# Expert stage: every low part on VectorE, a 16-bit one-hot, and gate and up weights loaded as pairs of rows

## The chip, the cores and the metric

One core of one Trainium2 chip runs the whole program in one launch. The metric is the device time of an execution in microseconds, as the median of the runs shown. TensorE multiplies, VectorE and ScalarE work on tiles in SBUF and PSUM, GpSimd works on tiles in SBUF and issues the indirect DMAs, SyncE issues the plain loads and stores. In the profile they are PE (with PEld for its weight loads), DVE, ACT, POOL and SP.

## The reference

Two encoder layers (`DEPTH = 2`) on 1024 tokens of 1024 features, all float32. Each layer has three sub-layers, each added to its scaled input and normalised: a parallel token mixer (grouped-query attention, a gated long convolution, latent attention), a cross-attention into 256 memory tokens, and the mixture of experts that this document is about:

```python
def expert_choice_moe(x, w_router, w_gate, w_up, w_down):
    cap = EC_FACTOR * n_tok // N_EXPERTS                        # 2 * 1024 // 16 = 128
    aff = jax.nn.softmax((x @ w_router).astype(jnp.float32), axis=-1)
    gates, idx = lax.top_k(aff.transpose(0, 2, 1), cap)         # each expert chooses 128 tokens
    xe = jax.vmap(lambda xb, ib: xb[ib])(x, idx)
    hid = jax.nn.silu(einsum(xe, w_gate)) * einsum(xe, w_up)    # [128, 1024] @ [1024, 512], twice
    ye = einsum(hid, w_down) * gates[..., None]                 # [128, 512] @ [512, 1024]
    return zeros.at[idx].add(ye)
```

Sixteen experts per layer; their weights (gate, up and down, 6 MB per expert) are each read once.

## The kernel before

Each float32 product is made of three passes over operands that are split exactly in two parts of 12 bits (`mm3`, L186): high x high, high x low, low x high. A `Weight` (L122) is a block of 512 KB: it is loaded by SyncE when it is made, and when first asked for (`get`) it is split: ScalarE copies it into the high part, and VectorE or GpSimd subtracts that from the raw block, which gives the low part (`split`, L174 to L177). The argument `le` says which of the two makes the low part.

An expert has eight blocks of gate and up (four units `u`, with `i` = 0 for gate and 1 for up, each 256 of the 1024 rows; two blocks of 128 rows lie side by side in a partition, `k` = 2) and four of down (two units of two blocks of 128 rows). `GP` and `DP` (L51, L52) give one of the eight and one of the four to GpSimd. `expert_units` (L1527) is the order of the blocks: gate and up 0, gate and up 1, down 0 of the expert before, gate and up 2, down 1 of the expert before, gate and up 3. The order of the instructions on TensorE, VectorE and ScalarE is the order in which the program writes them. `take` (L1575) hands out the next block; each call also splits the block that lies three (`SPLIT`, four from expert 8 on) ahead, and makes new blocks, that is, issues their loads, as long as the raw and split ones count less than 37 (`DEEP`). All these tiles share one pool of 41 buffers of 4 KB per partition (`NA`, `big`).

The tokens of an expert: `route` (L1457) leaves for every token and expert the slot 1 to 128, or 0 (`pos`). `chosen` (L1504) makes the one-hot [token, tile, slot] of an expert by comparing a row of slot numbers with `pos`. `pick` (L1512) multiplies it, as the stationary operand, by a payload of five columns (token tile, token, three parts of the affinity), and so finds the 128 token numbers (`ix`) and gates (`gt`). `gather` (L1555) then has GpSimd fetch the 128 rows by an indirect DMA. `turn` (L1570) transposes them in eight steps of TensorE (`turn_tile`, L1363) and splits them (`xt`). `gu` (L1585) multiplies, and makes the hidden values after unit 3; `hidden` (L1600) transposes and splits those (`ht`), one unit later; `down` (L1608) multiplies by down, scales by the gate and has GpSimd add the rows into DRAM by an indirect DMA.

In the loop over units, `chosen` for the expert after next comes first in unit 0, ahead of that unit's products and of `hidden`; `gather` for it comes behind unit 1, `turn` for the next expert behind unit 2 (L1644 to L1661).

`places` (L1561) uses the last expert's one-hot once more, at the end of the last layer.

Of the kernel before, what the change touches and what calls it, by code (L numbers as in the profile page):

```python
# [50 lines left out]
GP = lambda u, i: "p" if i and u == 1 else "v"  # L51
DP = lambda u, i: "p" if i and u else "v"  # L52
CHP = 0
TP = 0
# [18 lines left out]
# ---------------------------------------------------------------- constants of the shapes  # L73
# [47 lines left out]
# ---------------------------------------------------------------- the kernel  # L121
class Weight:  # L122
    """A block of weights: loaded when made, split in two parts when first asked for."""
# [15 lines left out]
class Net:  # L139
# [10 lines left out]
    # ---- tiles  # L150
# [22 lines left out]
    # ---- common steps  # L173
    def split(self, h, l, src, le="v"):  # L174
        """src = h + l exactly, each part of 12 bits."""
        self.nc.scalar.activation(h, src, AF.Copy)  # L176
        (self.nc.vector if le == "v" else self.nc.gpsimd).tensor_sub(l, src, h.bitcast(F32))  # L177
# [14 lines left out]
    def bcast(self, row, n, name):  # L192
        """A row of DRAM on every partition."""
        t = self.big((128, n), name=name) if n > 512 else self.cp.tile([128, n], F32, name=name, tag=name)
        self.nc.sync.dma_start(t, bass.AP(tensor=row.tensor, offset=row.offset, ap=[[0, 128], [1, n]]))
        return t
# [18 lines left out]
    def tables(self):  # L215
# [7 lines left out]
        self.iota = cp.tile([128, CAP], F32, name="iota")  # L223
        nc.sync.dma_start(self.iota, bass.AP(tensor=A["k_iota"].tensor, offset=A["k_iota"].offset, ap=[[0, 128], [1, CAP]]))
# [7 lines left out]
    # ---- activations to [feature, token], split  # L232
# [3 lines left out]
    def to_T(self, T, pair, xs):  # L236
        """Two token tiles into the split, transposed activations."""
# [23 lines left out]
    # ---- input projection  # L261
    def rms_rope(self, P, nt, nh, cs, up="p"):
        """P [128 tok, nt, nh * 64] in PSUM, nt * nh = 8 -> normed and rotated in SBUF; cs [128, nt, 2, 64] has the
        gain in."""
# [29 lines left out]
    def rope_gain(self, l):  # L294
        """Rotary tables with the norm's gain (and, for q, the score's scale) in."""
# [22 lines left out]
    def in_proj(self, l, T, fill=iter(())):  # L318
# [16 lines left out]
        # latents  # L335
# [42 lines left out]
        # gated convolution's branches, [channel, token]  # L378
# [45 lines left out]
        # keys and values, then queries  # L424
# [71 lines left out]
    def rope_small(self, dst, src, nh, t, eng=None):  # L496
        """Rotary of 32 features: dst, src [128, nh, 32]."""
# [13 lines left out]
    # ---- attention over the tokens  # L511
    def mix_dst(self, f, *halves):
        """The place of feature f in the mixed features: (partition, block of 128)."""
# [6 lines left out]
    def scores(self, passes):  # L520
        """One query tile's scores [query, key]."""
# [9 lines left out]
    def exps(self, S, nm, den):  # L531
        """exp(score - max) in SBUF, and its sums."""
# [13 lines left out]
    def values(self, O, PH, PL, rd, V, half):  # L546
        """[value features: (high | low), 256 queries | 1 / sums] in PSUM, in two steps."""
# [22 lines left out]
    def attention(self, n_pairs, pair, side, lead=3):  # L570
        """pair(n): (token pair, passes(t), V(kt), feature); scores run ahead of the products with the
        values; side(n) emits other work between."""
# [55 lines left out]
    def latents(self, l):  # L628
        """The latent heads' queries, keys and values, split, to DRAM."""
# [69 lines left out]
    def mla(self, l):  # L699
        """The latent heads' pairs, and the steps that bring their keys, values and queries back."""  # L700
# [36 lines left out]
    # ---- long convolution  # L737
    def sin_reduced(self, dst, P, freq, fb):
        """dst = sin(freq * (P + b)), the argument brought into [-pi, pi]; in steps."""
# [20 lines left out]
    def filter_mlp(self):  # L760
        """Both layers' filter networks: layer l on the partitions [64 l, 64 l + 64)."""
# [22 lines left out]
        # the last hidden values' two parts, one layer's on all the partitions: (high, low), (low, high)  # L784
# [22 lines left out]
    def dft_step(self, r, tabs, cH, cL, sH, sL, free=False):  # L807
        """[128 k, (cos | sin), k tile, 256]: cosine sums of one input, sine sums of the other."""
# [19 lines left out]
    def filter_spectra(self):  # L828
        """Both layers' filters by their networks' last hidden values, transformed, to DRAM."""
# [207 lines left out]
    # ---- projection, residual, layer norm  # L1037
    def stats(self, r, st, i):
        """The statistics of half a tile."""
# [22 lines left out]
    def out_weights(self, W, ks):  # L1062
        """Rows of an output projection, by blocks of 128."""
        return [Weight(self, W[k * 128:(k + 1) * 128, :], (128, 1024), "wo", "p" if k % 2 else "v") for k in ks]

    def split_pair(self, raw, p):
        """Two token tiles of the mixed features in two parts."""
# [8 lines left out]
    def proj_ln(self, raw, ws, res, g, b, emit, turned, per=2, bg=iter(())):  # L1076
        """emit(t, tile) for LayerNorm(alpha * res + raw^T @ W); turned(i) later, for the
        transposes of every per tiles."""
# [68 lines left out]
    # ---- cross attention  # L1147
# [7 lines left out]
    def mem_turned(self, ms):  # L1155
        """The memory, transposed and split."""
# [14 lines left out]
    def mem_k(self, l):  # L1171
        """The memory's keys [feature, memory], split, to DRAM."""
# [29 lines left out]
    def mem_v(self, l):  # L1202
        """The memory's values [memory, feature], split, to DRAM."""
# [158 lines left out]
    # ---- expert choice  # L1362
    def turn_tile(self, x, H, L, le="v"):  # L1363
        """A token tile, transposed and split, in two steps."""
        for g in range(2):
            pt = self.psT((128, 4, 128))
            for k in range(4):
                j = g * 4 + k
                self.nc.tensor.transpose(pt[:, k, :], x[:, j * 128:(j + 1) * 128], self.ident)  # L1369
# [12 lines left out]
    def router(self, w, X, t):  # L1382
        """Affinities [token, expert] of a token tile."""
# [21 lines left out]
    def combine(self, x, z, Y, X, rows, n, m):  # L1405
        """n pairs of runs of m in order, x's and z's, into runs of 2 * m, or of the largest CAP: in Y or X, the one
        that holds them first. X may be x."""
# [15 lines left out]
    def rank(self, t0, n, top=None):  # L1423
        """The largest CAP, in order, of n token tiles' affinities and of top: [expert, CAP]. Each quarter of the
        tokens is put in order on its own partitions."""
# [31 lines left out]
    def route(self, bg):  # L1457
        """From the affinities [token, tile, expert] each expert's CAP tokens: their slots (from 1) by token,
        0 for those not chosen, and the payload that finds token and gate."""
        nc, cp = self.nc, self.cp  # L1460
        aff = self.aff[:, :, 0:16]
        # payload: token tile, token, and the affinity in three exact parts
# [8 lines left out]
        # the smallest of the largest CAP  # L1471
# [11 lines left out]
        # those above it, and those at it, with their ranks by token: all of those above come first  # L1483
# [16 lines left out]
        self.pos = cp.tile([128, 8, 16], F32, name="pos", tag="pos")  # L1500
        nc.vector.tensor_tensor(self.pos, w[:, 0], w[:, 1], OP.add)
        yield

    def chosen(self, e):  # L1504
        """An expert's tokens, one-hot: [token, tile, slot]."""
        nc = self.nc
        oh = self.tp.tile([128, 8, CAP], BF16, tag="m", name="oh", bufs=3)
        (nc.gpsimd if CHP and e > 1 else nc.vector).tensor_tensor(oh, self.iota.unsqueeze(1).to_broadcast([128, 8, CAP]),
                                self.pos[:, :, e:e + 1].to_broadcast([128, 8, CAP]), OP.is_equal)
        return oh  # L1510

    def pick(self, e, oh):  # L1512
        """An expert's tokens and gates, [slot, 1]."""
        nc = self.nc
        P = self.psT((128, 8))
        for t in range(NT):
            nc.tensor.matmul(P[:, 0:5], oh[:, t, :], self.payload[:, t, e, :], start=t == 0, stop=t == NT - 1)
        v = self.sml(8, "pv")
        nc.scalar.activation(v[:, 0:5], P[:, 0:5], AF.Copy)
        ix = self.sp.tile([128, 1], U32, tag="ix", name="ix", bufs=6)  # L1520
        nc.vector.scalar_tensor_tensor(ix, v[:, 0:1], 128.0, v[:, 1:2], op0=OP.mult, op1=OP.add)
        gt = self.sp.tile([128, 1], F32, tag="gt", name="gt", bufs=6)
        nc.vector.tensor_tensor(gt, v[:, 2:3], v[:, 3:4], OP.add)
        nc.vector.tensor_tensor(gt, gt, v[:, 4:5], OP.add)  # L1524
# [414 lines left out]
```

## Time and profile before

| | us |
|---|---|
| median of three runs | 2776.77 |
| lowest, highest | 2771.78, 2776.84 |
| profiled execution, first to last instruction (its own time) | 2770.1 |
| TensorE busy, VectorE busy in it | 2576.6, 2006.3 |
| ScalarE busy, GpSimd busy | 1575.2, 989.5 |
| layer 1's expert stage, from expert 0's hidden transposes to expert 15's | 295.2 |
| layer 2's | 295.0 |

The profile records no separate device time for the profiled execution beside its span. The span lies 1.7 us below the lowest of the three runs and 6.7 below the median. Engine times are sums over the whole span. A row of the timeline is an instruction, or several alike that follow each other (xN): its start from the beginning of the span, its duration, the engine, the line, the operation, and out<-in by the program's names. Successive instructions of one engine overlap a little, so that what an instruction costs its engine is the distance from start to start. L176 and L177 are the helper `split`: its instructions are told apart by the tiles (`egh`, `egl` high and low part of a gate or up block, `edh`, `edl` of a down block, `xt` of the tokens, `ht` of the hidden values). TensorE's matmuls are pipelined and overlap by nearly half of what the profile shows as their duration.

### The profile page before, as it was taken

The page shows a single profiled execution, that of the slowest core. Times are in us where ns is not written, and L with a number is a line of the kernel's source. Part 1 is how long each engine was busy: PE and PEld are TensorE (multiplying, and loading weights), DVE is VectorE, ACT ScalarE, POOL GpSimd, SP SyncE. Part 2 cuts the span into 40 slices and gives each one's busy share as a digit, 9 for nine tenths or more (in the row PEclk, how much of TensorE's full clock was granted, in tenths as well). Part 3 has the DMA queues.
Part 4 walks back from the last instruction along what each step waited for, and adds up shares of the span by engine and source line. Part 5 has one row for each costly group of instructions (what it writes and reads, how often), then busy time and mean ns, then how long its engine had stood idle before and what let it go on. Part 6 is the DMA issues. An engine that isn't in the chain of part 4 may idle for free. (4 is left out here: it accounts for less than half of the span.)

```text
span 2770.1 us, 39879 instructions
## 1 busy us (share of the span) xinstructions
PE 2576.6 (93%) x14484; PEld 2153.2 (78%) x14484; DVE 2006.3 (72%) x3040; ACT 1575.2 (57%) x2740; POOL 989.5 (36%) x831
## 2 busy tenths in 40 slices
PE   7999989999999995999989998999989999599998
PEld 5788879888778884777779887988977888477775
DVE  6665568877643578999976556887765357899997
ACT  4533359878223444787754425887831344377775
POOL 2443428742201201444451333774230130144444
PEclk9999999999999997999999999999999999799999
DMA  7546110233223357999885611024322235799994
GB/s 200 176 162 205 39 46 31 92 99 115 83 78 101 99 199 264 347 376 358 298 255 165 220 47 46 30 94 99 84 84 99 85 98 183 253 348 369 363 315 152
DMA packets 224566, 468.05 MB, mean 169 GB/s; under 512 B 27001, under 2 KB 83919, under 8 KB 224368
## 3 DMA queue, kind: packets, MB, share of 16 engines
q1 hardware_dynamic: 197504, 369.32, 38.5%
q0 software_dynamic: 22256, 79.40, 10.4%
q10 hardware_dynamic: 4608, 16.78, 1.5%
q8 instruction: 114, 1.87, 0.3%
q14 instruction: 84, 0.69, 0.1%
HBM read 378.66 MB, written 86.77 MB: 168 GB/s over the span
## 5 line engine op out<-in xcount | busy, mean ns | idle before, releaser
L177 DVE TENSOR_TENSOR egl<-eg,egh 128x1024 fp32r<-128x1024 f32 x224 | 315.4, 1436 | 32.7 <-ACT egh L176 27.2
L176 ACT ACTIVATE egh<-eg 128x1024 fp32r<-128x1024 f32 x256 | 267.8, 1058 | 82.4 <-DVE edl L177 40.9
L528 DVE TENSOR_REDUCE nm<-S 128x1 f32<-128x1024 f32 x192 | 234.1, 1221 | 96.6 <-PE S L525 95.6
L177 DVE TENSOR_TENSOR PL<-T,PH 128x512 fp32r<-128x512 f32 x384 | 246.0, 682 | 17.5 <-ACT PH L176 15.4
L176 ACT ACTIVATE PH<-T 128x512 fp32r<-128x512 f32 x384 | 209.8, 595 | 80.4 <-PE T L542 79.3
L534 ACT ACTIVATE E<-S,nm 128x1024 f32<-128x1024 f32 x192 | 214.5, 1117 | 11.5 <-DVE nm L528 9.6
L189 PE MATMUL S<-egl,xt 128*128 128x512 f32 x512 | 206.9, 404 | 8.6 <-DVE egl L177 6.3
L188 PE MATMUL S<-woh,mh 128*128 128x512 f32 x512 | 207.7, 406 | 6.3 <-DVE r L1107 6.3
L542 PE MATMUL T<-ident,E 128*128 128x128 f32 x1536 | 204.5, 274 | 5.7 <-DVE PL L177 4.8
L542 PEld LDWEIGHTS T<-ident,E 128*128 128x128 f32 x1536 | 178.2, 141 | 40.1 <-DVE PL L177 14.9
L189 PE MATMUL S<-wol,mh 128*128 128x512 f32 x512 | 202.2, 395 | 3.7 <-POOL wol L177 2.5
L188 PE MATMUL S<-egh,xt 128*128 128x512 f32 x512 | 204.9, 400 | 0.0
L190 PE MATMUL S<-egh,xt 128*128 128x512 f32 x512 | 201.5, 394 | 0.0
L190 PE MATMUL S<-woh,ml 128*128 128x512 f32 x512 | 201.3, 393 | 0.0
L567 POOL TENSOR_TENSOR olo<-olo 64x256 f32<-64x256 f32 x96 | 70.2, 731 | 290.5 <-ACT olo L565 286.6
L1616 PE MATMUL O<-edh,ht 128*128 128x512 f32 x512 | 156.9, 409 | 13.4 <-DVE ht L177 12.0
L525 PE MATMUL S<-KS,QS 128*128 128x512 f32 x512 | 147.1, 411 | 0.7 <-ACT E L534 0.7
L176 ACT ACTIVATE edh<-ed 128x1024 fp32r<-128x1024 f32 x128 | 133.6, 1055 | 23.1 <-PE O L1616 16.6
L552 PE MATMUL O<-PH,VS 128*128 128x256 f32 x512 | 137.9, 302 | 0.0
L189 PEld LDWEIGHTS S<-egl,xt 128*128 128x128 f32 x512 | 97.0, 189 | 47.3 <-DVE egl L177 21.5
L177 DVE TENSOR_TENSOR edl<-ed,edh 128x1024 fp32r<-128x1024 f32 x96 | 129.1, 1359 | 1.2 <-ACT edh L176 1.0
L1558 POOL DMA_INDIRECT xg<-x2d,ix x32 | 54.6, 1705 | 208.0 <-DVE gt L1524 121.4
(410 smaller groups left out, 7371.6 us busy)
## 6 DMA issues: line engine op xcount, KB each, us to landing
eg<-moe_w_gate SPq DMA_DIRECT2D x128, 512.0 KB, 8.1
eg<-moe_w_up SPq DMA_DIRECT2D x128, 512.0 KB, 8.8
ed<-moe_w_down SPq DMA_DIRECT2D x128, 512.0 KB, 5.6
tab<-k_dft POOLq DMA_DIRECT2D x24, 512.0 KB, 4.6
wv<-xa_wkv SPq DMA_DIRECT2D x16, 512.0 KB
wk<-xa_wkv SPq DMA_DIRECT2D x16, 512.0 KB, 6.6
tab<-k_idft POOLq DMA_DIRECT2D x16, 512.0 KB, 4.7
wo<-w_o SPq DMA_DIRECT2D x16, 512.0 KB, 3.6
```

The source lines that it names most:

```text
L176: self.nc.scalar.activation(h, src, AF.Copy)
L177: (self.nc.vector if le == "v" else self.nc.gpsimd).tensor_sub(l, src, h.bitcast(F32))
L188: mm(out, ah, bh, start=start, stop=False)
L189: mm(out, ah, bl, start=False, stop=False)
L190: mm(out, al, bh, start=False, stop=stop)
L525: self.nc.tensor.matmul(S[:, hf * 512:hf * 512 + 512], a, b[hf], start=n == 0, stop=n == len(passes) - 1)
L528: self.nc.vector.tensor_reduce(nm, S, axis=AX.X, op=OP.max, negate=True)
L534: self.nc.scalar.activation(E, S, AF.Exp, bias=nm, scale=1.0, accum_out=den)
L542: self.nc.tensor.transpose(pt[:, k, :], P[:, kt * 128:(kt + 1) * 128], self.ident)
L552: nc.tensor.matmul(O[:, :256], v, PH[half][:, k, :], start=kt == 0, stop=False)
L567: nc.gpsimd.tensor_tensor(lo[s, 0], lo[s, 0], lo[s, 1], OP.add)
L1616: nc.tensor.matmul(O[e][n], a[:, 2 * u + f, :], w[:, n * 512:n * 512 + 512], start=s, stop=z)
```

## The change

Four things change, all in the expert stage:

- `GP` and `DP` go; the low part of every block of expert weights is made by VectorE.
- The slot numbers (`iota`, each written twice side by side) and `pos` become bfloat16 tiles, laid out so that the one-hot is [token, slot, tile] with pairs of tiles as the innermost dimension of all three operands. The picks (and `places`) take their stationary operand from it with a step of eight elements. The gate is summed by ScalarE (`accum_out`) and no longer by two additions on VectorE. `chosen` moves behind `hidden` in unit 0.
- A partition of a gate or up block holds two neighbouring rows (`(p k) n`, 4 KB in DRAM) in place of two rows 128 apart (`(k p) n`, 2 KB each).
- To match, `turn_tile` with `pairs` takes every second feature of 256 for a transpose.

```diff
-GP = lambda u, i: "p" if i and u == 1 else "v"
-DP = lambda u, i: "p" if i and u else "v"
...
-        self.iota = cp.tile([128, CAP], F32, name="iota")
-        nc.sync.dma_start(self.iota, bass.AP(tensor=A["k_iota"].tensor, offset=A["k_iota"].offset, ap=[[0, 128], [1, CAP]]))
+        iota = self.tmp((128, CAP), name="iota")
+        nc.sync.dma_start(iota, bass.AP(tensor=A["k_iota"].tensor, offset=A["k_iota"].offset, ap=[[0, 128], [1, CAP]]))
+        self.iota = cp.tile([128, CAP, 2], BF16, name="iotab")
+        nc.vector.tensor_copy(self.iota, iota.unsqueeze(2).to_broadcast([128, CAP, 2]))
...
-    def turn_tile(self, x, H, L, le="v"):
+    def turn_tile(self, x, H, L, le="v", pairs=False):
...
-                self.nc.tensor.transpose(pt[:, k, :], x[:, j * 128:(j + 1) * 128], self.ident)
+                if pairs:
+                    a = x[:, j // 2 * 256:j // 2 * 256 + 256].rearrange("p (m k) -> p k m", k=2)[:, j % 2, :]
+                else:
+                    a = x[:, j * 128:(j + 1) * 128]
+                self.nc.tensor.transpose(pt[:, k, :], a, self.ident)
...
-        self.pos = cp.tile([128, 8, 16], F32, name="pos", tag="pos")
-        nc.vector.tensor_tensor(self.pos, w[:, 0], w[:, 1], OP.add)
+        self.pos = cp.tile([128, 16, 8], BF16, name="pos", tag="pos")
+        nc.vector.tensor_tensor(self.pos.rearrange("p e t -> p t e"), w[:, 0], w[:, 1], OP.add)
...
-        oh = self.tp.tile([128, 8, CAP], BF16, tag="m", name="oh", bufs=3)
-        (nc.gpsimd if CHP and e > 1 else nc.vector).tensor_tensor(oh, self.iota.unsqueeze(1).to_broadcast([128, 8, CAP]),
-                                self.pos[:, :, e:e + 1].to_broadcast([128, 8, CAP]), OP.is_equal)
+        oh = self.tp.tile([128, CAP, 8], BF16, tag="m", name="oh", bufs=3)
+        sh = [128, CAP, 4, 2]
+        self.nc.vector.tensor_tensor(oh.rearrange("p s (a b) -> p s a b", b=2), self.iota.unsqueeze(2).to_broadcast(sh),
+                                     self.pos[:, e:e + 1, :].rearrange("p o (a b) -> p o a b", b=2).to_broadcast(sh), OP.is_equal)
...
-            nc.tensor.matmul(P[:, 0:5], oh[:, t, :], self.payload[:, t, e, :], start=t == 0, stop=t == NT - 1)
+            nc.tensor.matmul(P[:, 0:5], oh[:, :, t], self.payload[:, t, e, :], start=t == 0, stop=t == NT - 1)
...
-        nc.scalar.activation(v[:, 0:5], P[:, 0:5], AF.Copy)
+        gt = self.sp.tile([128, 1], F32, tag="gt", name="gt", bufs=6)
+        nc.scalar.activation(v[:, 0:2], P[:, 0:2], AF.Copy)
+        nc.scalar.activation(v[:, 2:5], P[:, 2:5], AF.Copy, accum_out=gt)
...
-        gt = self.sp.tile([128, 1], F32, tag="gt", name="gt", bufs=6)
-        nc.vector.tensor_tensor(gt, v[:, 2:3], v[:, 3:4], OP.add)
-        nc.vector.tensor_tensor(gt, gt, v[:, 4:5], OP.add)
...
-                    v = self.A[("moe_w_gate", "moe_w_up")[i]][l, e, r, :].rearrange("(k p) n -> p k n", p=128)
-                    w = Weight(self, v, (128, 2, 512), "eg", GP(u, i))
+                    v = self.A[("moe_w_gate", "moe_w_up")[i]][l, e, r, :].rearrange("(p k) n -> p k n", k=2)
+                    w = Weight(self, v, (128, 2, 512), "eg")
...
-                    w = Weight(self, v, (128, 1024), "ed", DP(u, i))
+                    w = Weight(self, v, (128, 1024), "ed")
...
-            drain(self.turn_tile(xg, *X[e], "p" if e and TP else "v"))
+            drain(self.turn_tile(xg, *X[e], pairs=True))
...
-                if u == 0 and e + 2 < NE:
-                    oh = self.chosen(e + 2)
                 if l == DEPTH - 1 and (e, u) == PLC:
                     places(oh)
                 gu(e, u)
                 if u == 0 and e:
                     hidden(e - 1)
+                if u == 0 and e + 2 < NE:
+                    oh = self.chosen(e + 2)
```

`places` takes `oh[:, :, 4 * g + i]` in the same way. Comments and docstrings are dropped, which moves the line numbers.

## Rows read from the trace of the kernel before

**Rows 1.** The page's slices: DMA's mean busy share in tenths, 40 slices.
```profile
DMA  7546110233223357999885611024322235799994
```

**Rows 2.** Sums by stretch: length; engines' busy us; granted clock, DMA share, GB/s.
```profile
1146.00:1244.60 98.60, 97.43 (x460) 71.36 (x460) 91.93 (x91) 77.76 (x96) 42.42 (x21) 1.00 1.05 374
1285.30:1365.70 80.40, 75.41 (x369) 58.34 (x369) 77.65 (x73) 61.92 (x77) 37.97 (x17) 1.00 1.02 357
...
1106.10:1401.30 295.20, 282.68 (x1352) 214.71 (x1352) 280.04 (x262) 230.87 (x284) 132.47 (x59) 1.00 0.97 337
```

**Rows 3.** Timeline of TensorE within one expert: start us, duration us, instruction.
```profile
1202.02 0.40 PE L190 MATMUL S<-egh,xt 128*128 128x512 f32 x1
...
1204.77 0.39 PE L190 MATMUL S<-egh,xt 128*128 128x512 f32 x1
1205.19 0.66 PE L1603 MATMUL T<-ident,hid 128*128 128x128 f32 x4
1205.60 0.47 PE L188 MATMUL S<-egh,xt 128*128 128x512 f32 x1
1205.91 0.39 PE L189 MATMUL S<-egl,xt 128*128 128x512 f32 x1
...
1208.57 0.35 PE L1517 MATMUL T<-payload,oh 128*128 128x5 bf16 x8
1208.78 0.71 PE L1616 MATMUL O<-edh,ht 128*128 128x512 f32 x2
...
1215.17 1.04 PE L1369 MATMUL T<-ident,xg 128*128 128x128 f32 x8
1215.96 0.71 PE L1616 MATMUL O<-edh,ht 128*128 128x512 f32 x2
```

**Rows 4.** Timeline of VectorE within the same expert.
```profile
1205.05 3.27 DVE L1508 TENSOR_TENSOR oh<-iota,pos 128x1024 bf16<-128x1024 f32 x1
1208.24 1.21 DVE L177 TENSOR_TENSOR edl<-ed,edh 128x1024 fp32r<-128x1024 f32 x1
1209.37 0.68 DVE L177 TENSOR_TENSOR ht<-T,ht 128x512 fp32r<-128x512 f32 x1
...
1216.22 2.08 DVE L177 TENSOR_TENSOR egl<-eg,egh 128x1024 fp32r<-128x1024 f32 x1 [1.26 <-ACT egh L176]
```

**Rows 5.** Timeline of GpSimd within the same expert.
```profile
1204.84 2.39 POOL L177 TENSOR_TENSOR egl<-eg,egh 128x1024 fp32r<-128x1024 f32 x1 [1.34 <-ACT egh L176]
...
1214.77 2.44 POOL L177 TENSOR_TENSOR edl<-ed,edh 128x1024 fp32r<-128x1024 f32 x1
```

**Rows 6.** Waits: us, times, longest. TensorE 1285.3:1365.7, ScalarE 1146.0:1244.6.
```profile
PE O L1616 <- DVE ht L177: 3.9, 4, 1.0
...
ACT egh L176 <- DVE edl L177: 10.4, 5, 2.1
...
ACT egh L176 <- DMA eg<-moe_w_gate: 0.6, 2, 0.3
```

**Rows 7.** DMA of 1194.6:1197.6 (2 KB packets) and of 1191.4:1192.9 (4 KB).
```profile
DMA packets 612, 1.18 MB, mean 394 GB/s; under 512 B 35, under 2 KB 35, under 8 KB 612
...
DMA packets 189, 0.62 MB, mean 411 GB/s; under 512 B 21, under 2 KB 21, under 8 KB 189
```

**Rows 8.** Line 957 (step of four elements): count, duration ns min/median/max.
```profile
L957 PEld LDWEIGHTS T<-ident,zx x32: 195/213/220, 368.9 to 1725.6; 128*128 128x128 f32 x32
L957 PE MATMUL T<-ident,zx x32: 283/286/387, 368.9 to 1725.7; 128*128 128x128 f32 x32
```

**Rows 9.** Timeline of TensorE: two successive transposes of line 957.
```profile
369.10 0.41 PE L957 MATMUL T<-ident,zx 128*128 128x128 f32 x2
```

**Rows 10.** Timelines of VectorE, GpSimd and TensorE at the stage's start.
```profile
1080.16 2.36 DVE L1508 TENSOR_TENSOR oh<-iota,pos 128x1024 bf16<-128x1024 f32 x2
...
1082.88 1.04 POOL L1558 DMA_INDIRECT xg<-x2d,ix  x1 [19.18 <-DVE gt L1524]
...
1087.62 1.94 PE L1369 MATMUL T<-ident,xg 128*128 128x128 f32 x8 [4.66 <-DMA xg<-x2d,ix]
```

More of the change, by code (lines that the diff above doesn't have):

```diff
@@ L50 @@
 DEEP = lambda e: 37
-GP = lambda u, i: "p" if i and u == 1 else "v"
-DP = lambda u, i: "p" if i and u else "v"
-CHP = 0
-TP = 0
 MV1 = 1
@@ L1499, in route @@
         nc.vector.tensor_tensor(w[:, 1], w[:, 1], C[:, 1], OP.mult)
-        self.pos = cp.tile([128, 8, 16], F32, name="pos", tag="pos")
-        nc.vector.tensor_tensor(self.pos, w[:, 0], w[:, 1], OP.add)
+        self.pos = cp.tile([128, 16, 8], BF16, name="pos", tag="pos")
+        nc.vector.tensor_tensor(self.pos.rearrange("p e t -> p t e"), w[:, 0], w[:, 1], OP.add)
         yield
     def chosen(self, e):
-        nc = self.nc
-        oh = self.tp.tile([128, 8, CAP], BF16, tag="m", name="oh", bufs=3)
-        (nc.gpsimd if CHP and e > 1 else nc.vector).tensor_tensor(oh, self.iota.unsqueeze(1).to_broadcast([128, 8, CAP]),
-                                self.pos[:, :, e:e + 1].to_broadcast([128, 8, CAP]), OP.is_equal)
+        oh = self.tp.tile([128, CAP, 8], BF16, tag="m", name="oh", bufs=3)
+        sh = [128, CAP, 4, 2]
+        self.nc.vector.tensor_tensor(oh.rearrange("p s (a b) -> p s a b", b=2), self.iota.unsqueeze(2).to_broadcast(sh),
+                                     self.pos[:, e:e + 1, :].rearrange("p o (a b) -> p o a b", b=2).to_broadcast(sh), OP.is_equal)
         return oh
@@ L1566, in places @@
                 for i in range(4):
-                    nc.tensor.matmul(pt[:, i, :], oh[:, 4 * g + i, :], ib, start=True, stop=True)
+                    nc.tensor.matmul(pt[:, i, :], oh[:, :, 4 * g + i], ib, start=True, stop=True)
                 nc.scalar.activation(self.place[:, 4 * g:4 * g + 4, :], pt, AF.Copy)
```

## The prediction

> **What bounds the kernel now.** Only the expert stage of the two layers is touched. I read the page's slices, then the sums by stretch, then each engine's timeline over one expert, then the waits and the DMA.
>
> The slices place the stage: the DMA line of [rows 1] is full twice, once per layer. The sums [rows 2] run from one expert's hidden transposes to a later one's: expert 2 to 7 (first row: five periods of 98.60/5 = 19.72 us) and 9 to 13 (second row: four of 80.40/4 = 20.10 us). In the first kind TensorE is busy 97.43 of 98.60, VectorE 91.93, DMA share 1.05; in the second VectorE 77.65 of 80.40. The layer's 15 periods take 295.20 (third row); the second layer repeats the pattern. So three resources are near full, and the question is who waits for whom.
>
> TensorE's own work is in [rows 3]. Twelve starts of 512-column matmuls lie 1204.77-1202.02 = 2.75 apart, 0.229 each; an expert has 48 for gate and up and 24 for down, 72 x 0.229 = 16.5. Eight token transposes take 1215.96-1215.17 = 0.79, four hidden ones 1205.60-1205.19 = 0.41, the eight small matmuls that pick the tokens 1208.78-1208.57 = 0.21. The first matmul after each of these three starts some 0.08 late (1205.60 to 1205.91 is 0.31, not 0.23): 0.25. Sum 18.16. Hence TensorE waits 1.56 per period in the first kind and 1.94 in the second, and none of its columns changes.
>
> What it waits for is VectorE: the wait list of the second kind [rows 6] has 3.9 us in four waits on the hidden's low part (`ht`). The timeline shows why [rows 4]: the one-hot (`oh`) takes 3.27 and stands ahead of the low parts of down and `ht`. The same low part that takes 1.21 alone takes 2.08 elsewhere. Both slow ones lie beside a GpSimd low part [rows 5] (1204.84 to 1207.23, and 1214.77 to 1217.21); none of the 1.21 ones does. The first one-hots of the stage, with GpSimd idle, take 2.36 for two [rows 10]. So GpSimd's 2.39 us per low part are paid by VectorE too.
>
> DMA is full as well, but ScalarE, the first reader of a weight block, waits for a landing 0.6 us in 98.6 against 10.4 for VectorE [rows 6]. By the code 37 - 2 - 2 x 3, some 29 blocks of raw weights, are issued ahead, 2.4 experts, so DMA may fall behind by tens of microseconds in the stage before anyone starves.
>
> **Low parts to VectorE.** Two of twelve blocks per expert move. On VectorE they cost 1209.37-1208.24 = 1.13 each from start to start: +2.26. Relief: the second `egl` falls from 2.08 to 1.21, -0.87; the one-hot beside an idle GpSimd falls from 3.27 to 1.18 (2.36/2), -2.1, before its width is counted. Together -0.7 on VectorE. GpSimd keeps only its indirect DMAs, which now queue behind nothing there. Latency: the moved blocks were ready 2.39 after their high part, now 1.21.
>
> **16-bit one-hot.** No row has a two-input operation on 16-bit data throughout. Upper bound: no faster than today alone, 1.18. Lower bound: the price of half the elements, 0.68 for `ht` [rows 4]. I take 0.7, as both operands are made in neighbouring pairs; the difference of 0.5 is covered as long as VectorE has room. Two gate additions on single columns leave VectorE (not counted); ScalarE gets one small activation and an accumulator read, below 0.4 by my estimate, on an engine that is busy 77.76/5 = 15.6 of 19.72 [rows 2]. The one-hot now comes after `ht`, so `ht` and the first down block no longer queue behind it; behind the one-hot stand the second down block and a gate block, due some 2 us later. VectorE's sum becomes 12 x 1.13 + 5 half-size ones (`xt` twice, `ht`, `hid`, one-hot) x 0.6 (0.68 less the same overlap) + 0.1 = 16.7, against 18.4 now (91.93/5).
>
> **Pairs of rows.** For 512 KB in 2 KB packets the DMA moved 394 GB/s, in 4 KB packets 411 [rows 7]. Gate and up are 4.19 MB per expert: 10.65 to 10.2 us, -0.45 of DMA time, off the path unless DMA paces. [...]
>
> The tokens must match, so the eight transposes load every second element, and the picks load every eighth 16-bit element. The nearest row reads every fourth fp32 element: a `zx` load takes 213 ns and its transpose 286 [rows 8]; two such transposes together take 0.41 [rows 9], so start to start 0.41-0.286 = 0.12, against 0.79/7 = 0.11 for today's. Mostly hidden, then: +0.1 for the transposes. For the picks, 26 ns apart today, the bounds are 0 and 8 x (0.213-0.026) = 1.5; I take +0.1 by the hidden case. [...]
>
> **Sum.** TensorE's own work becomes 18.16 + 0.2 = 18.36. With VectorE at 16.7 I walked one expert through the queues by these durations: every low part is ready 0.5 to 2 us before its matmul. Some waits will stay, since ScalarE may only split a block when TensorE has freed the tiles of the one four earlier; I leave a quarter of today's 1.56, 0.4. Period 18.75. Thirteen of a layer's 15 periods are full ones: they take 259.6 now (295.20 less the last two, 35.6), then 13 x 18.75 + 0.4 for the first = 244.2, -15.4. The last two have no one-hot and no pick: -0.8. At the start two one-hots become 1.2 shorter and the index no longer waits for the gate sums: the gather of 1082.88 starts 1.1 earlier, and TensorE stands 4.66 waiting for it [rows 10], so this counts in full; the first expert loses its own slow low parts, -0.5. Per layer -17.8, two layers -35.6. The profiled execution's 2770.1 becomes 2734.5. That span is 6.7 under the median of the runs; I take the saving off the median: 2776.8 - 35.6 = 2741.
>
> **Rivals.** (a) *Nothing is left waiting* and strided loads cost nothing: 18.2 per period, -0.55 x 13 more per layer, 2726. For it: all deadlines are met on paper; against: ScalarE and VectorE stay at some 90%.
>
> (b) *DMA paces the stage.* For it: a share above 1 in both stretches [rows 2]; against: ScalarE's 0.6 us of waits and the long lead. Then only the packets count: -0.45 x 15 x 2 - 3.2 at the starts = -17: 2760.
>
> (c) *DMA paces it and packet size gives nothing*, or TensorE and ScalarE hold the period by the free tiles: only the starts remain, 2773. [...] ScalarE's 10.4 us of waits for tiles freed by VectorE speak for a loop of tiles, but VectorE is what gets shorter.
>
> (d) *The strided 16-bit load is exposed.* The pick has five columns, nothing to hide a load behind. At 213 ns for each of 16 strided loads against 26 and 110: 8 x 0.187 + 8 x 0.103 = 2.3 per expert on TensorE, the engine that sets the period. The period is then 18.75 - 0.2 + 2.3 = 20.85, against 19.9 on average today: 13 x 0.95 x 2 = +25, less 3 at the starts and 2 at the ends: 2797. It decides from 1.35 per expert on, 84 ns per strided load. Against it: the `zx` cadence.
>
> [...]
>
> **How the numbers follow.** Forecast with (e) 0.54, 2741, own range 2728 to 2755; (a) 0.10; (b) 0.20; (c) 0.06; (d) 0.10. The range 2724 to 2766 holds the forecast, (a) and (b) with their edges, and leaves out (c), (d) and a little of (a). A measurement here can't tell less than 0.2% (5.5 us) from no change, so 2771 to 2782 is same: faster 0.84, same 0.06, slower 0.10.
>
> **What would show it.** Right: periods near 18.75 between hidden transposes in both kinds; no 2 to 3 us operation on VectorE; one-hot near 0.7; TensorE's waits on `ht` gone; packets of 2 KB gone from the stage. DMA landings may come later without ScalarE waiting; if ScalarE waits for them, (b). Wrong: the eight picks over 1 us, or the transposes over 1.2, is (d); a period of 19.3 with full DMA is (b). I would be wrong altogether if the low parts on VectorE stayed at 1.4 on average with GpSimd idle.

## The result, and the profile after

The changed kernel takes 2757.47 us in the median (2754.68 to 2759.00, four runs), the kernel before 2774.28 on the same chip (2771.28 to 2776.84, four runs): ratio 0.9942, 95% interval 0.9927 to 0.9956, so 16.8 us less. In the profiled executions the span goes from 2770.1 to 2755.4. The direction was right and the time lies in the range; the saving is less than half of the 35.6 forecast, and the time is within 3 us of the 2760 that rival (b) gave.

The sums by stretch answer to [rows 2] (same columns: length, busy time of TensorE, its weight loads, VectorE, ScalarE, GpSimd, then clock, DMA share, GB/s). As there, the stretches run from one expert's hidden transposes to a later one's.

```profile
1144.60:1240.70 96.10, 94.28 (x460) 75.65 (x460) 85.45 (x91) 77.42 (x106) 17.33 (x10) 1.00 1.03 385
1280.40:1357.20 76.80, 75.12 (x369) 60.81 (x369) 68.25 (x73) 62.38 (x85) 13.87 (x8) 1.00 1.03 378
1105.86:1392.22 286.36, 277.60 (x1353) 224.59 (x1353) 255.21 (x267) 231.21 (x310) 47.28 (x28) 1.00 0.97 349
```

The period is 96.10/5 = 19.22 and 76.80/4 = 19.20 us, for 19.72 and 20.10 before; the forecast was 18.75. VectorE is busy 17.1 us of it, as intended (16.7 forecast), and GpSimd has only its transfers left. The groups of VectorE over the first layer's 15 periods show both parts at work (shape, count, busy time, mean ns, idle before; two groups of the kernel before come first): no low part is slow any more, and the one-hot takes 680 ns where 2939 was its mean before.

```profile
L177 DVE TENSOR_TENSOR egl<-eg,egh 128x1024 fp32r<-128x1024 f32 x100 | 142.1, 1449 | 13.7 <-ACT egh L176 12.0 <-DMA eg<-moe_w_gate 1.3
...
L1508 DVE TENSOR_TENSOR oh<-iota,pos 128x1024 bf16<-128x1024 f32 x13 | 38.2, 2939 | 0.0
```

```profile
L173 DVE TENSOR_TENSOR egl<-eg,egh 128x1024 fp32r<-128x1024 f32 x117 | 140.1, 1221 | 21.6 <-ACT egh L172 17.1 <-DMA eg<-moe_w_gate 2.6
L173 DVE TENSOR_TENSOR edl<-ed,edh 128x1024 fp32r<-128x1024 f32 x64 | 76.5, 1219 | 9.2 <-ACT edh L172 9.2
...
L1510 DVE TENSOR_TENSOR oh<-iotab,pos 128x1024 bf16<-128x1024 bf16 x13 | 8.8, 680 | 0.0
```

So VectorE idles, the DMA share is still above 1, and the period is 0.47 over the forecast. TensorE's timeline within one expert, answering to [rows 3], shows where:

```profile
1201.61 0.40 PE L186 MATMUL S<-egh,xt 128*128 128x512 f32 x1
1202.31 0.66 PE L1604 MATMUL T<-ident,hid 128*128 128x128 f32 x4 [0.30 <-DVE hid L1598]
1202.72 0.47 PE L184 MATMUL S<-egh,xt 128*128 128x512 f32 x1
...
1205.34 0.39 PE L186 MATMUL S<-egh,xt 128*128 128x512 f32 x1
1205.78 0.65 PE L1519 MATMUL T<-payload,oh 128*128 128x5 bf16 x8
1206.29 0.71 PE L1617 MATMUL O<-edh,ht 128*128 128x512 f32 x2
```

Three things are longer than they need be. The hidden transposes start 0.70 after the last product, where products follow each other by 0.23: 0.47 of waiting. The picks start 0.44 after theirs: 0.21. And the eight picks take 1206.29 - 1205.78 = 0.51, for 0.21 in [rows 3]. VectorE and ScalarE within the same expert:

```profile
1199.30 2.36 DVE L173 TENSOR_TENSOR egl<-eg,egh 128x1024 fp32r<-128x1024 f32 x2 [0.88 <-ACT egh L172]
1201.58 0.68 DVE L1598 TENSOR_TENSOR hid<-hid,S 128x512 f32<-128x512 f32 x1
...
1203.31 1.22 DVE L173 TENSOR_TENSOR edl<-ed,edh 128x1024 fp32r<-128x1024 f32 x1
1204.44 0.68 DVE L173 TENSOR_TENSOR ht<-T,ht 128x512 fp32r<-128x512 f32 x1
1205.05 0.68 DVE L1510 TENSOR_TENSOR oh<-iotab,pos 128x1024 bf16<-128x1024 bf16 x1
```

```profile
1198.21 2.00 ACT L172 ACTIVATE egh<-eg 128x1024 fp32r<-128x1024 f32 x2
1200.11 0.59 ACT L1597 ACTIVATE hid<-S 128x512 f32<-128x512 f32 x1
```

The one-hot ends at 1205.73, the picks start at 1205.78: its new place behind `ht` is too late for them. And `hid` stands behind two low parts on VectorE, its silu behind two splits on ScalarE. The wait list of experts 2 to 7 has the same two, as waits of TensorE's weight loads (us in total, times, longest):

```profile
PEld T L1604 <- DVE hid L1598: 3.7, 5, 0.7
PEld L1519 <- DVE oh L1510: 2.4, 5, 0.5
```

### The profile page after: what moved, and what is told of

Same layout as the page of the kernel before. It is cut to its first block, busy times and chain, and to the rows that moved or that the text cites. A ratio compares the mean times of both kernels' runs of the same rounds, so it can differ in the third digit from the quotient of the medians.

```text
span 2755.4 us, 39814 instructions
## 1 busy us (share of the span) xinstructions
PE 2573.3 (93%) x14484; PEld 2179.1 (79%) x14484; DVE 1952.9 (71%) x3041; ACT 1577.7 (57%) x2804; POOL 810.8 (29%) x767
## 4 chain that ended last, share of the span: by engine, by line
PE 69%; DVE 14%; DMA 6%; ACT 5%; issue 5%; POOL 1%; SPq 0%; DVEq 0%; ACTq 0%; POOLq 0%
PE S L184 7%; PE S L185 7%; PE S L186 7%; PE S L523 6%; PE T L540 5%; PE O L184 5%; PE O L186 5%; PE O L185 5%; PE O L1617 5%; PE S L417 4%; PE O L551 3%; PE O L550 3%; DMA eg<-moe_w_up 2%; DMA eg<-moe_w_gate 2%; DVE rk L1420 1%
## 5 line engine op out<-in xcount | busy, mean ns | idle before, releaser
L173 DVE TENSOR_TENSOR egl<-eg,egh 128x1024 fp32r<-128x1024 f32 x256 | 306.8, 1221 | 52.0 <-ACT egh L172 43.3
L185 PE MATMUL S<-egl,xt 128*128 128x512 f32 x512 | 200.6, 392 | 0.0
L173 DVE TENSOR_TENSOR edl<-ed,edh 128x1024 fp32r<-128x1024 f32 x128 | 153.1, 1219 | 18.5 <-ACT edh L172 18.5
L551 PE MATMUL O<-PL,VS 128*128 128x256 f32 x512 | 127.2, 282 | 0.0
```

Source lines behind the costliest of these rows:

```text
L185: mm(out, ah, bl, start=False, stop=False)
L551: nc.tensor.matmul(O[:, :256], v, PL[half][:, k, :], start=False, stop=kt == 7)
```

## The experiments

The question: does TensorE pace the stage by its own work and these waits (theory T), or do the transfers (theory D, the forecast's rival (b), whose 2760 came close)? Times are medians; ratios are to the kernel before, run beside it on the same chip. Periods are lengths between hidden transposes, over five periods of experts 2 to 7 and four of 9 to 13, in the first layer.

| kernel | us | ratio, 95% interval | period 2-7 | 9-13 |
|---|---|---|---|---|
| before | 2769.6 to 2774.3 | 1 | 19.72 | 20.10 |
| changed | 2757.47 | 0.9942, 0.9927-0.9956 | 19.21 | 19.20 |
| e1 changed, rows of 2 KB | 2755.13 | 0.9940, 0.9923-0.9956 | 19.11 | 19.08 |
| e2 changed, 28% fewer bytes | 2758.07 | 0.9951, 0.9935-0.9968 | 19.23 | 19.22 |
| e3 silu between the halves | 2805.36 | 1.0112, 1.0094-1.0130 | 20.96 | 21.05 |
| e4 the same, and one-hot | 2801.58 | 1.0109, 1.0092-1.0126 | 20.35 | 20.58 |
| e5 silu behind both halves | 2751.06 | 0.9940, 0.9919-0.9961 | 19.20 | 19.21 |
| e6 the same, and one-hot | 2729.15 | 0.9858, 0.9841-0.9874 | 18.45 | 18.28 |
| e7 before, low parts alone | 2745.88 | 0.9925, 0.9906-0.9944 | 18.86 | 19.08 |
| e8 one-hot part alone | 2784.45 | 1.0053, 1.0034-1.0072 | 20.28 | 20.69 |
| e9 changed, one-hot by slots | 2750.48 | 0.9919, 0.9903-0.9936 | 18.92 | 18.89 |
| e10 changed, one-hot earlier | 2752.36 | 0.9931, 0.9914-0.9948 | 18.99 | 19.50 |
| e11 e6, four ahead, one memory step | 2724.66 | 0.9828, 0.9812-0.9845 | 18.27 | 18.26 |
| e12 e11, rows of 2 KB | 2724.74 | 0.9831, 0.9815-0.9847 | 18.19 | 18.18 |
| e13 e7, silu as in e5 | 2740.67 | 0.9895, 0.9878-0.9911 | 18.88 | 18.72 |
| e14 e13, four ahead | 2740.87 | 0.9892, 0.9875-0.9908 | 18.72 | 18.72 |

**Do the transfers pace? (e1, e2)**

```diff
-  v = ...[l, e, r, :].rearrange("(p k) n -> p k n", k=2)      # e1
+  v = ...[l, e, r, :].rearrange("(k p) n -> p k n", p=128)
-  drain(self.turn_tile(xg, *X[e], pairs=True))
+  drain(self.turn_tile(xg, *X[e], pairs=False))
-  net.nc.sync.dma_start(self.raw, view)                       # e2, gate and up
+  net.nc.sync.dma_start(self.raw[:, 0:1, :], view[:, 0:1, :])
+  self.raw = self.raw[:, 0:1, :].to_broadcast(list(shape))
```

> The changed kernel with its gate and up blocks loaded by rows of 2 KB again (and the tokens turned without the step of two); all else stays. Theory T (TensorE paces: its own work and what it waits for VectorE's hid and one-hot make the 19.22 us of a period; the transfers could deliver more): the period stays 19.2 us and the time 2757 within 3 us. Rival D (the transfers pace, 7.37 MB an expert at about 385 GB/s): the smaller packets take 85 to 88 ns for 2 KB where 4 KB took 159 to 162 ns, some 7% more per byte on two thirds of the bytes, so the period goes to 19.7 to 20.0 us and the time up by 12 to 20 us, to 2769 to 2777.

> The changed kernel with only the first of each two rows of a gate or up block loaded, read twice by the splits: 2.1 MB of the 7.37 MB an expert are left out (half of the gate and up weights is replaced by their neighbours), the instructions on the engines stay. T: the DMA share falls to some 0.75 and the period stays 19.2 us, the time 2757 within 3 us. D: the period falls to what TensorE needs without late data, about 18.5 us, and the time by some 19 us, to 2738.

The sums by stretch of e1, then of e2:

```profile
1144.60:1240.70 96.10, 94.11 (x463) 75.38 (x464) 85.81 (x92) 77.92 (x107) 17.36 (x10) 1.00 1.05 374
1280.40:1357.20 76.80, 75.09 (x371) 60.70 (x371) 68.61 (x74) 62.66 (x85) 13.87 (x8) 1.00 1.04 375
```

```profile
1144.60:1240.70 96.10, 94.31 (x461) 75.69 (x460) 85.41 (x91) 77.32 (x106) 17.38 (x10) 1.00 0.91 274
1280.40:1357.20 76.80, 75.22 (x368) 60.85 (x368) 68.28 (x73) 61.83 (x85) 13.87 (x8) 1.00 0.86 276
```

D falls on both sides. With 2 KB rows the DMA moves 374 GB/s in place of 385 and the period is not longer but 0.1 shorter; with a good quarter of the bytes gone (274 GB/s) it stays to 0.02 (the share fell to 0.91 and 0.86 only, in packets of 2 KB). The pairs of rows gave nothing, and their matching transposes (eight at 108 ns for 99) cost 0.07 of the 0.1. That the forecast's rival (b) gave 2760 was a coincidence.

**Can hid's wait be taken away alone? (e3, e4, e5)**

```diff
   for i in range(2):
-      h, lo = take(e)                    # own block, and split the blocks ahead
+      h, lo = take(e, u < 3 or i == 0)   # the last one: own block only
       ...
+      if u == 3 and i == 0:              # e3, e4: silu here
+          nc.scalar.activation(H[e], P[e][:, 0:512], AF.Silu)
   if u == 3:
-      nc.scalar.activation(H[e], P[e][:, 0:512], AF.Silu)    # e5: stays here
       nc.vector.tensor_tensor(H[e], H[e], P.pop(e)[:, 512:1024], OP.mult)
+      ready(e)                           # split the blocks ahead now
```

> The changed kernel with the silu put right behind the gate half of an expert's last gate-up step and the two-part splits ahead of time that stood between put behind the product hid: hid is made before ScalarE's and VectorE's next splits. T: the wait of the hidden transposes for hid (0.47 us in experts 2 to 7, 0.60 in 9 to 13) goes, so the period falls by 0.4 to 0.55 us to about 18.75, and the ends of the layers, where TensorE waited 2.1 and 2.4 us for the last hid and its clock then fell to the lower level, save 1 to 3 us each: 2740 to 2744 in all. D: the period stays 19.2 us, with another wait in hid's place; only the ends save: 2752 to 2755.

> As the kernel with the early silu; besides, the one-hot is made a step earlier (behind the last gate-up step of the expert before), and it is laid out slot by slot for each token tile, so that a pick's matmul loads its stationary side from neighbouring elements (the positions are stored twice each, so that VectorE's innermost step stays of two 16-bit elements). T: beside hid's wait the picks' 0.2 us wait for the one-hot goes, and the eight picks go from 62 back to 26 ns each (0.3 us): period about 18.25 us, time 2725 to 2732. D: period 19.2 us, time 2752 to 2755.

Both became some 30 us slower than before. TensorE's wait list of e3, experts 2 to 7, names a new wait, five times 1.9 us (e4's has the same):

```profile
PE S L184 <- ACT hid L1601: 9.6, 5, 1.9
```

Gate and up sums share the tile `S`; a silu issued between the two halves is waited for by the up half, though it reads only the gate's columns. So these two runs say nothing of T or D. I mended the place:

> The changed kernel again with the silu moved, but behind both halves of the last gate-up step, where it was; only the one split ahead that the up half called for goes behind the product hid instead of in front of the silu. Theory T1 (in the kernel with the early silu TensorE's up half waited for the silu on the shared tile of sums, 1.9 us an expert, and that alone made it slower): silu about 0.7 us earlier than in the changed kernel, hid ready before its transposes, no wait of TensorE on ScalarE's silu; period 18.7 to 18.85 us, time 2741 to 2746. Rival T2 (ScalarE and VectorE, with their splits in a ring of tiles that TensorE frees, hold the period, so that a split put later is paid for in full): period 19.2 us or more, time 2755 to 2775.

T1's explanation of e3 held (that wait is gone), its forecast did not: the period is 19.20, as in the changed kernel and as T2 said, and the 2751.06 lies between the two. But the waits are not T2's ring of tiles: hid's left TensorE's list, and the picks' wait for the one-hot, 0.21 in the changed kernel, grew by about as much (they start 1.01 after the last product, where 0.23 is usual, so 0.78):

```profile
1170.01 0.39 PE L186 MATMUL S<-egh,xt 128*128 128x512 f32 x1
1171.02 0.66 PE L1519 MATMUL T<-payload,oh 128*128 128x5 bf16 x8 [0.62 <-DVE oh L1510]
```

`hid`, the low parts behind it, `ht` and the one-hot are one chain on VectorE. Without the first wait TensorE comes sooner to the second.

**Both waits and the layout. (e6, e9, e10)** The one-hot's place and its layout, together with e5's silu in e6, each alone in e9 and e10:

```diff
-  if u == 0 and e + 2 < NE:              # e6, e10: made a step earlier
-      oh = self.chosen(e + 2)
+  if e < 13 and u == 3:
+      oh = self.chosen(e + 3)
-  oh = self.tp.tile([128, CAP, 8], BF16, ...)    # e6, e9: [token, tile, slot]
+  oh = self.tp.tile([128, 8, CAP], BF16, ...)    # pos is stored twice, iota once
-  mm(P[:, 0:5], oh[:, :, t], ...)
+  mm(P[:, 0:5], oh[:, t, :], ...)
```

> That kernel with the one-hot a step earlier and laid out slot by slot. T1: a period of about 18.25 us, picks back at 26 ns each, time 2726 to 2734. T2: period 18.9 to 19.2 us (the picks' 0.3 us may come back as another wait), time 2748 to 2756.

> The changed kernel with the one-hot laid out slot by slot for each token tile, so that the picks load neighbouring 16-bit elements; all else stays, its place behind ht too. Theory P (the strided load costs TensorE 0.31 us an expert, eight picks of 62 ns for 26, on the path): picks at 26 ns, period 18.9 us, time some 8 to 9 us less than the changed kernel, 2747 to 2750. Rival P0 (the cost is covered: the waits for the one-hot and hid grow by what the picks lose): period 19.2 us, time 2755 to 2758.

> The changed kernel with the one-hot made a step earlier, behind the last gate-up step of the expert before, so that it stands ahead of ht and of two low parts again; its layout stays strided. Theory Q (the one-hot's new place, behind ht, holds the picks): the picks' wait of 0.2 us for it goes; hid's wait of 0.47 stays or grows by a little, since the one-hot now stands near hid: period 18.95 to 19.1 us, time 2750 to 2755. Rival Q0 (VectorE's sum is what counts, not the order): period 19.2 us, time 2755 to 2758.

T1 holds for e6: 2729.15, and TensorE's busy time fills its stretch (73.78 of 73.80 us in four periods of 18.45):

```profile
1162.90:1236.70 73.80, 73.78 (x370) 59.41 (x369) 68.32 (x73) 62.34 (x85) 11.36 (x8) 1.00 1.03 385
```

In e9 (P right) the eight picks are back at the 0.35 us of [rows 3], for 0.65 in the changed kernel, and the period is shorter by the whole 0.30. TensorE's timeline of e9:

```profile
1186.71 0.35 PE L1521 MATMUL T<-payload,oh 128*128 128x5 bf16 x8
```

In e10 Q is right for experts 2 to 7 (18.99, 0.22 less). In experts 9 to 13, where four blocks are split ahead, hid's wait grew instead (3.6 us in four, for 1.8 in the changed kernel) and the period to 19.50; neither theory had that. e7, below, with the old one-hot in its old place, has the same wait there (0.9 at the longest in both), so the new one-hot is not its cause; why this order suits three blocks ahead and not four I did not settle.

**Which part of the change carries the gain? (e7, e8)**

```diff
-GP = lambda u, i: "p" if i and u == 1 else "v"      # e7, in the kernel before
-DP = lambda u, i: "p" if i and u else "v"
+GP = lambda u, i: "v"
+DP = lambda u, i: "v"
-  w = Weight(self, v, (128, 2, 512), "eg")          # e8, in e1's kernel
+  w = Weight(self, v, (128, 2, 512), "eg", "p" if i and u == 1 else "v")
-  w = Weight(self, v, (128, 1024), "ed")
+  w = Weight(self, v, (128, 1024), "ed", "p" if i and u else "v")
```

> The kernel before with one part of the change alone: VectorE makes all low parts; the one-hot is the old one, the rows are 2 KB. By the forecast's sums VectorE has 18.4 + 2.3 - 0.9 - 2.1 = 17.7 us an expert; the one-hot (1.2 us, in 32-bit) still stands ahead of ht. T (both parts take from VectorE what TensorE waits for): period 19.4 to 19.6, time 2760 to 2768, that is some half of the gain. Rival L (the slow two-input operations beside GpSimd were all of it, the 16-bit one-hot nothing): period 19.2, time 2754 to 2758. Rival O (the one-hot is all): no faster than before, 2770 or more.

> The other part alone: the 16-bit one-hot behind ht, the gate by accumulation, the picks from the strided layout; GpSimd keeps its two low parts an expert and the rows are 2 KB. T: VectorE 18.4 - 2.1 = 16.3 us an expert (the one-hot perhaps 1.0 beside GpSimd, slow low parts of 2.08 stay): period 19.3 to 19.5, time 2758 to 2765. L: no faster than 2768. O: 2752 to 2757, all of the gain.

T and O missed both times; L had only the sign of e8 right (no faster than 2768). The low parts alone give more (24 us) than the whole change (16.8), since the other parts bring to TensorE what e7 does not have: 0.30 us an expert for the strided picks, 0.21 of waiting for the one-hot and 0.07 for the transposes (e7 in turn waits some 0.26 more for low parts of gate and up, so its period is 0.35 shorter). The one-hot part alone loses 15. In e8 the picks wait for the one-hot 0.9 us an expert (first row), because VectorE's low parts beside GpSimd are still slow (second row) and now stand ahead of it:

```profile
PE T L1519 <- DVE oh L1510: 4.3, 5, 0.9
```

```profile
L173 DVE TENSOR_TENSOR edl<-ed,edh 128x1024 fp32r<-128x1024 f32 x15 | 25.3, 1689 | 2.7 <-ACT edh L172 2.7
```

**The best version. (e11, e12)**

```diff
-SPLIT = lambda e: 3 if e < 8 else 4
+SPLIT = lambda e: 3 if e < 1 else 4
-MEMX = {94: 2, 95: 3, 96: 3}
+MEMX = {94: 1, 95: 4, 96: 3}
```

> The kernel of all four (silu ahead of one split, one-hot earlier and slot by slot) with two more: four blocks split ahead from the second expert on, in place of three up to the eighth, and one step of the next layer's memory transposes between the last gate-up step and the last hidden transposes, in place of two. From that kernel's 2729: experts 2 to 7 go from 18.44 to the 18.28 of experts 9 to 13 and the jump of 0.5 at expert 8 goes, some 1.9 a layer; in the first layer the last hidden transposes no longer wait 2.6 us for the memory's low part, and TensorE's clock stays up behind them: 2 to 4 us. Sum: 2720 to 2726. Rival: four ahead from the start frees tiles later for the loads and costs as much as it saves: 2727 to 2732.

> The same with gate and up loaded by rows of 2 KB and the tokens turned without the step of two. Theory T (the transfers have room even now, the step of two costs TensorE 0.1 us an expert): period 18.2 us, 2 to 4 us below the kernel with pairs of rows. Rival D2 (at a period of 18.3 us the transfers of 2 KB, which moved 374 GB/s when they were always in flight, fall behind over the stage until the splits wait for landings): the later experts of each layer at 18.6 to 19.6 us with ScalarE waiting for DMA, 3 to 15 us above the kernel with pairs.

Both reach 2724.7, some 48 us under the kernel before and the fastest here. The sums of e12's two stretches:

```profile
1146.17:1237.14 90.97, 90.97 (x461) 73.88 (x460) 84.91 (x91) 78.00 (x106) 33.60 (x10) 1.00 1.05 373
1273.53:1346.24 72.71, 72.71 (x369) 59.11 (x368) 67.88 (x73) 62.39 (x85) 26.87 (x8) 1.00 1.05 373
```

TensorE is busy throughout, 18.19 us an expert: the 18.16 of [rows 3] with nothing waited for. D2 falls: at 373 GB/s only 6.8 MB arrive per period of the 7.4 an expert needs (36.96 MB in the changed kernel's five), and still TensorE waits for nothing and ScalarE for two landings of 0.5 us in the two stretches. The blocks loaded ahead last to the end of the layer; by my estimate 15 periods fall short by 15 x 0.6 = 9 MB, of the 29 x 0.52 = 15 MB that are issued ahead. T's period held (0.08 below e11), its 2 to 4 us do not show in the medians. Four blocks ahead did what was expected; the memory step did not: the first layer's last hidden transposes came 2 us sooner, and in e11 the clock behind them fell all the same (granted 0.57 and 0.58), in e12 it did not (below).

**Is the 16-bit one-hot worth anything? (e13, e14)** e5's silu edit and e11's `SPLIT`, put on e7.

> The kernel before with all low parts on VectorE and the silu ahead of one split, nothing else: the 32-bit one-hot of 1.2 us in its old place ahead of ht, slot by slot, rows of 2 KB. With the low parts alone the period was 18.86 and 19.10 us, 0.5 to 0.7 of it the wait for hid. Theory N (the 16-bit one-hot is worth nothing once the low parts are on VectorE and hid is early): period 18.25 to 18.45 us, time 2727 to 2733. Rival M (the 32-bit one-hot then stands in the way of ht or of the picks, and hid's wait comes back there): period 18.6 to 18.9 us, time 2737 to 2746.

> The same with four blocks split ahead from the second expert on. N: period 18.2 us throughout, as in the kernel of everything with rows of 2 KB, time 2722 to 2728. M: 18.5 to 18.9 us, time 2735 to 2746.

M is right: 18.72 for 18.2. The 32-bit one-hot of 1.22 us stands ahead of `ht`, and the down products wait for `ht`, 0.4 each time. TensorE's waits of e14, five and four periods (in e13's experts 2 to 7, with three blocks ahead, it waits 0.5 an expert for a gate block's low part instead):

```profile
PE O L1621 <- DVE ht L177: 2.0, 5, 0.4
...
PE O L1621 <- DVE ht L177: 1.6, 4, 0.4
```

Against e12's 18.19, the short one-hot, laid out slot by slot and made a step earlier, is worth 0.5 us an expert. How much of that is its width and how much its place is not shown: no run has the 32-bit one-hot a step earlier.

## Why the prediction was partly wrong

- **What bounds the stage** was right: TensorE with its waits for VectorE, and full DMA with a long lead that binds nobody (e1, e2, e12). TensorE's own 18.16 was right to 0.03.
- **Low parts to VectorE** was right: 1.22 each, no slow ones, VectorE 17.1 for 16.7 (the prediction's own steps, 18.4 - 0.7 - 0.5, give 17.2), ScalarE unchanged (77.42 for 77.76 us in five periods; the small activation and the accumulator read take 0.17 and 0.20 an expert). Alone it brings 24 us.
- **Pairs of rows at nothing on the path** was right: the rates differ, 385 against 374 GB/s, and the period is no shorter for it, 19.21 against 19.11 us in e1.
- **The strided picks were mis-sized**: 0.1 taken between bounds of 0 and 1.5, 0.30 measured (62 ns for 26, e9). The fp32 transposes from which I took the hidden case have 128 columns, the picks five; I take that to be why their loads show, but no run varied the columns. This is (d)'s mechanism at a small size: 0.30 for the picks and 0.07 for the transposes, of the 2.3 that (d) counted and the 1.35 from which it decided (36 and 9 ns more a load, for 84). The transposes' own 0.1 was about right: 108 ns each for 99 (the prediction's 0.79/7 = 0.11 should be 0.79/8).
- **The step that failed is the one-hot's new place.** I looked at what stands behind the one-hot on VectorE (`ht` freed, two low parts due later) and not at the one-hot's own reader: the picks stand right there in TensorE's order and wait 0.21 (e10 gains 0.22 in experts 2 to 7; in 9 to 13, `hid` then waits longer). At expert 8 the fourth block split ahead puts one more low part in front of `ht` and the one-hot, and the picks wait 1.2 us. That is the longest wait in TensorE's list over the first layer's 15 periods:

```profile
PE T L1519 <- DVE oh L1510: 1.6, 2, 1.2
```

- **"A quarter of today's waits, 0.4"** was an allowance, not a wait with a name. What stayed is 0.47 on `hid` and 0.21 on the one-hot, 0.68, and e5 shows them to be one chain. I had walked the low parts through the queues, but not `hid`, which has low parts in front of it.
- **Per period**: 18.16 + 0.30 (picks) + 0.07 (transposes) + 0.68 = 19.21, for 18.75. Over experts 0 to 13 the two layers save 8.3 and 8.6 us, each forecast at 15.4. Of the 7.0 missing per layer 13 x 0.46 = 6.0 is this; the rest is the period at expert 8 (20.44, 1.2 above its neighbours), where the picks wait for the one-hot. e10, with the one-hot earlier, has 19.55 there, and e11, with four blocks ahead from the second expert on, 18.27: no jump. I had counted it as a usual period.
- **Starts and ends**: forecast -4.8, measured +2.2 (the span's -14.7, less the -16.9 of the periods). The gather stands 2.85 us behind the start of `pos`, for 3.04: 0.2 sooner, not 1.1, since the write of `pos` took 0.72 us for 0.29 and the strided picks part of the rest. First row before, then the changed kernel:

```profile
1079.84 0.29 DVE L1501 TENSOR_TENSOR pos<-rk 128x128 f32<-128x128 f32 x1
```

```profile
1079.59 0.72 DVE L1503 TENSOR_TENSOR pos<-rk 128x128 bf16<-128x128 f32 x1
```

- At a layer's end, from the last hidden transposes to the start of the last down product, 1.6 and 1.1 us were lost (7.60 to 9.19 and 8.33 to 9.45). In front of these transposes TensorE waited for VectorE, 2.1 us in the first layer for 1.2 before, 2.4 in the second for 1.5. That comes with the low parts that GpSimd made: with the low parts alone (e7) the two waits are 2.1 and 2.4 as well, with the one-hot part alone (e8) 1.2 and 1.5. In the first layer TensorE's granted clock then fell to 0.50 and 0.65 of full speed for the down products, where the kernel before kept 1.00; in the second layer it fell in both, to 0.50 here and to 0.52 and 0.63 in the kernel before. The wait is not shown to be the cause: e9 and e10 have the same 2.1 us in the first layer and kept the full clock (1.00 in e9's rows below), and there the end takes 7.60 and 7.58, as before. So the 1.6 goes with the clock of the profiled execution, not with the wait. The granted clock is the column before the last two; first layer, before, after and e9:

```profile
1401.00:1403.00 2.00, 0.98 (x5) 0.72 (x6) 1.22 (x3) 0.60 (x1) 1.15 (x1) 1.00 0.95 307
1403.00:1405.00 2.00, 2.00 (x10) 1.64 (x9) 0.35 (x1) 0.00 (x0) 0.00 (x0) 1.00 1.03 258
```

```profile
1394.00:1396.00 2.00, 2.00 (x7) 1.53 (x6) 0.23 (x1) 0.00 (x0) 0.00 (x0) 0.50 1.03 208
1396.00:1398.00 2.00, 2.00 (x7) 1.55 (x6) 0.00 (x0) 0.00 (x0) 0.00 (x0) 0.65 0.06 10
```

```profile
1391.70:1393.70 2.00, 2.00 (x11) 1.61 (x10) 0.00 (x0) 0.00 (x0) 0.00 (x0) 1.00 0.97 195
1393.70:1395.70 2.00, 2.00 (x15) 1.74 (x14) 0.56 (x1) 1.19 (x3) 0.00 (x0) 1.00 0.05 8
```

- **Rivals**: (b) falls by e1 and e2, and so does the first half of (c); its second half, the ring of tiles, would have left 2773. (e), a one-hot no faster than the old one alone (1.18 us), falls by the 680 ns; (a) did not happen here but is what e12 reaches; (d) was there at a small price. The prediction's sign "a period of 19.3 with full DMA is (b)" was no test: 19.2 with full DMA came about by two waits and a slow load.

## What to carry to other kernels

When an operation is moved in a queue, look first at who reads its result and when, and only then at what stands behind it. A resource at a share of 1 with a deep lead proves nothing: take bytes away and look whether the period moves (in e2, with 28% fewer, it stayed to 0.02 us). Waits that hang on one engine's queue did not add here: taking the earlier one away gave nothing (e5), taking the later one away gave its 0.22 in one half of the stage and cost 0.3 in the other (e10), and taking both away together with the slow load gave 0.77 of the 0.98 (e6), with a fourth block ahead 0.94 (e11).

## What was not expected of the hardware

- Matmuls of five columns whose stationary side is loaded from 16-bit elements at a step of 16 bytes start 62 ns apart; from neighbouring elements 26 (e9).
- A write of 128 16-bit elements per partition at a step, out of 32-bit sums, took VectorE 0.72 us, the 32-bit write in order 0.29.
- A comparison of 1024 16-bit elements per partition with pairs innermost takes VectorE 0.68 us, as much as 512 fp32 ones; the one on 32-bit data takes 1.22 with GpSimd idle (e14) and 2.94 in the mean in the kernel before, where GpSimd makes low parts beside it.
- The clock's fall at a layer's end does not follow from the waits in front of it. After a wait of 2.1 us and one of 0.7 it fell in the changed kernel's first layer (granted 0.50 and 0.65 of full speed in two stretches of 2 us), and it stayed in e9 and e10. After 2.6 and 0.7 it stayed in e5; after 1.5 and 0.7 it fell in the second layer of the kernel before (0.52 and 0.63). After 1.0 and 0.7 it fell in e11 (0.57 and 0.58) and stayed in e12. With the same waits in front, the first layer's end differs by 1.6 us by this alone (9.19 for 7.60 in e9). What decides it stays open, and the saving of a few us at such a place can't be forecast from its wait.
